# The rows of ten units by way of DRAM instead of one-hot products

## The chip, the cores and the metric

The kernel runs on one core of a Trainium2 chip. The metric is the time of one execution on the device, in microseconds, as the median of several runs. TensorE multiplies matrices, VectorE and ScalarE work on elements, GpSimd (POOL) does the same more slowly and issues the indirect DMAs, SyncE (SP) issues most of the other transfers. 16 DMA engines move the data of all queues.

## The reference

Two blocks follow each other on 512 tokens of 1024 channels. Each has a mixer and then a mixture of experts. The change is in the first block's mixture: 32 experts in four groups, two experts of one group for each token.

```python
def hier_moe(x2d, w_grp, b_grp, w_exp, b_exp, w_gate, w_up, w_down):
    ...
    combine = jnp.sum(jax.nn.one_hot(global_idx, N_EXPERTS, dtype=jnp.float32) * weights[..., None], axis=1)
    y = jnp.zeros_like(x2d)
    for e in range(N_EXPERTS):
        h = jax.nn.silu(x2d @ w_gate[e]) * (x2d @ w_up[e])
        y = y + combine[:, e:e + 1] * (h @ w_down[e])
    return y
...
xn = rmsnorm(h, norm_ffn_g[l]).reshape(B * S, D)
y = hier_moe(xn, ...)
h = h + y.reshape(B, S, D)
```

## The kernel before

The kernel runs in four stages: `mixer1`, `moe1`, `mixer2`, `moe2`. The tokens' sum `h` stays in SBUF as four tiles of [128 tokens, 1024]. A build step gives each engine one fixed order of its instructions. It takes those that are ready first, by a model of their times, so an instruction may stand well ahead of its place in the text; `in_order` keeps the written order for some stretches.

**The first mixture** (`moe1`, L1626). Two experts are one unit; there are 16 units. An expert has 64 slots, a unit 128. The routing (`route`, `tables`) leaves for each slot the number of its token (`mo.num` as float32, `mo.idx` as an integer) and its weight (`mo.wts`); empty slots have a number out of range. In `body` (L1646) a unit does this:

- `gather` (L1578): GpSimd issues an indirect DMA that fetches the tokens' normed rows from DRAM (`xd`) into one of two tiles `xg`, two units ahead.
- `gathered`: TensorE transposes them, ScalarE copies them out (`xTh`).
- The hidden layer (L1673): 64 products with the weights of gate and up, then Silu and a product (`hh`), transposed again by `turned`.
- `down` (L1633), one unit late: 16 products (L1641) with the down weights into PSUM. `rows_hl` (L1736) evicts them, times the slots' weights, as a high part on ScalarE and a low part on VectorE; `onehot` (L1741) makes the matrix slot by token.
- `scatter` (L1746): the rows of two units go to `h`, one half of the columns in each of two later units: 16 products with the one-hot matrices (`scatter_mm`, L1759 and L1760) and four adds on `h` (L1753) for a half. In units 3 to 14 there is one such half each; what is left follows in and after the last unit.

The weights come in pieces of 1 MB, six for a unit (`moe_load`, L1526), in the order of use, into a ring of 17 places. SyncE issues a piece when the piece that had its place has been used. After the 16 units a loop does further rounds, if an expert has more than 64 tokens; ahead of it all engines meet. Then the last unit's rows are added (`end`), and the norms of the next block follow (`sums_two`).

**Where the second mixture has the like.** There, the rows of 14 units go to a DRAM array `yd` (L1828), and eight indirect DMAs (L1885) bring them back into SBUF at the end; `places` (L1419) makes the row numbers. The first mixture does not call it.

**The first mixer.** `mixer1` (L438) loads the projections' weights piece by piece on SyncE (`wload`, L282), and the LoRA weights `lw` (L528). In step P0 of its list `sb_proj` (L635) makes `qz`, and GpSimd clears half of the partitions of each half of it (L638, L639).

Of the kernel before, what the change touches and what calls it, by code (L numbers as in the profile page):

```python
# [8 lines left out]
F32 = mybir.dt.float32  # L9
# [7 lines left out]
T = 512  # L17
D = 1024
NT = 4
# [7 lines left out]
BYDRAM = 14  # L27
ZROW = BYDRAM * 96
# [3 lines left out]
def drain(gen):  # L32
    """what a generator returns"""
    while True:
        try:
            next(gen)
        except StopIteration as e:
            return e.value


class Layout:
    """Columns of the packed constant arrays, one array per part of the program."""
# [19 lines left out]
    "mo1": (("cap64", 8), ("sl64", 128), ("g_f1", 8)),  # L62
    "mo2": (("cap96", 8), ("sl96", 128), ("g_f2", 8), ("row", 16)),
# [3 lines left out]
def host_consts(inp):  # L67
# [27 lines left out]
    # numbers of tokens, less 4096, as sums of two that bfloat16 holds  # L95
# [3 lines left out]
    put("row", one * np.where(np.arange(16) < BYDRAM, 96 * np.arange(16), 1e5))  # L99
# [22 lines left out]
def pieces(w, width=256):  # L122
    """[1024, n*width] -> [n, 128, 8*width], row d = k*128+p."""
    w = np.asarray(w)
    d, n = w.shape
    return np.ascontiguousarray(
        w.reshape(d // 128, 128, n // width, width).transpose(2, 1, 0, 3)).reshape(n // width, 128, -1)
# [50 lines left out]
class Kern:  # L178
# [16 lines left out]
    def act_set(self, name, after=None):  # L195
        """switch ScalarE's function table; what follows on ScalarE stays behind it"""
# [12 lines left out]
    def in_order(self):  # L209
        """every engine issues what is written here in the order in which it is written"""  # L210
# [19 lines left out]
    def cbf(self, pool, name):  # L230
        """a constant in bfloat16"""
# [21 lines left out]
    def psum(self, **banks):  # L253
        """new division of the 8 PSUM banks"""
# [12 lines left out]
    def ps_names(self, **names):  # L267
        """further names, each for banks in turn"""
# [6 lines left out]
    def rot(self, tags):  # L275
        """the next bank from a cycle of tags"""
# [8 lines left out]
    def wsplit(self, pool, t, w, bufs=2, eng=None):  # L285
        """a piece [128, 8, w] as hi + lo"""
# [11 lines left out]
    def proj_plan(self, w, order):  # L298
        """pieces of the weights that projections will ask for"""
# [27 lines left out]
    def rsqrt(self, pool, dst, src, scale, eps, tag):  # L327
        """dst = (src*scale + eps)^-0.5"""
# [5 lines left out]
    def to_dT(self, n, xn, xh, xl, diag=None, halfway=None):  # L334
        """a tile [128 tok, d], times a diagonal if there is one, transposed as hi + lo"""
# [21 lines left out]
    def norm_in(self, pool, pp, x, xh, xl):  # L357
        """rmsnorm of the input, transposed, and the first projection: of its first half while the second is on its way"""
# [27 lines left out]
    def sums_two(self, room, junk):  # L386
        """What norm_two needs. With w = h*g1 and a = mean(h^2) + eps, the result is w*g2*(mean(w^2) + eps*a)^-0.5.
        GpSimdE and VectorE take two tiles each; for GpSimdE's, the factors go on diagonals.
        room: a [128, 2 * d] for each tile of tokens, for w, and w*g2; junk: another"""
# [33 lines left out]
    def norm_two(self, xh, xl):  # L423
        """rmsnorm(rmsnorm(h)*g1)*g2, transposed"""
# [3 lines left out]
    def norm_h(self, pool):  # L428
        """h = rmsnorm(h)*g1, the first block's output"""
# [8 lines left out]
    def mixer1(self, after):  # L438
# [51 lines left out]
        # P projections and A attention of a pair of heads, R a unit of RWKV-7: one's products fill the other's waits  # L490
        for step in "R00 R01 P0 R10 R11 A0 P1 R20 R21 A1 P2 R30 R31 A2 P3 A3".split():
            kind, j = step[0], int(step[1])
            if kind == "P":
                qkv[j] = self.sb_proj(pp, sp, j, xh, xl)
                if j == 3:
# [20 lines left out]
    def wo_load(self, w):  # L516
        """the output projection's weights, in the ring of the mixture that follows: pieces on their way"""
# [5 lines left out]
    def mixer1_rw_in(self, bp, wk, pp, first, xh, xl, AR, bt, kt, vch, xg, TTc, PC, lora):  # L523
# [34 lines left out]
        for j in range(4):  # L558
# [8 lines left out]
            # key  # L567
# [19 lines left out]
            # k*(1+(a-1)*k_a)  # L587
# [4 lines left out]
            # receptance  # L592
# [5 lines left out]
            # L = strict(A~ b~^T), transposed blocks  # L598
# [9 lines left out]
        # (I - L)^-1 of 128 32x32 matrices, one per lane  # L608
# [15 lines left out]
    def to_tok(self, pool, p, dst, tag):  # L624
        """channel-major psum [128 ch, 512 tok] -> token-major [128, NT, 128]"""
# [54 lines left out]
    def blocks(self, scores, weighted):  # L680
        """the blocks of queries, the scores of one ahead of the products of the one before"""
# [6 lines left out]
    def weighted(self, tp, tags, b, w, v, ot):  # L688
        """ot[2 heads x 64, block b] = (w v)^T for weights [128 tok, keys]"""
# [18 lines left out]
    def head_norm(self, tp, tags, ot, dst, g):  # L708
        """rmsnorm of [2 heads x 64, 512 tok] over each head's channels"""
# [9 lines left out]
    def rw_unit(self, up, n, g, S, o, AR, bt, kt, vch, xg, g2, TTc, PC):  # L719
        """RWKV-7 for 128 tokens of 4 heads (2 pairs); in three steps: what needs no state, the chain, the output"""  # L720
# [9 lines left out]
        # products, s on partitions  # L730
# [21 lines left out]
        # token-major copies  # L752
# [24 lines left out]
        # [W | U0]  # L777
# [10 lines left out]
        # R' = R~ + M_rb W (transposed), M = I + W^T b~  # L788
# [15 lines left out]
        # chain over the 4 chunks  # L804
# [23 lines left out]
        # group norm, bonus, gate  # L828
# [32 lines left out]
    def out_mm(self, st, d, n, k, hl, first, last):  # L861
        """one row chunk of the product for 128 tokens and 256 columns, into half a bank"""
# [22 lines left out]
    def out_start(self, o, wo, ks, rest, tags, cx):  # L885
        """three quarters of the output projection's columns over the rows that are there already"""
# [21 lines left out]
    def out_finish(self, st, tag, trtag, rtags):  # L908
        """the rest of the output projection; with the last columns rmsnorm(h) to DRAM, and the routing"""
# [99 lines left out]
        with self.tc.issue_after(ins.ins):  # L1009
# [4 lines left out]
            if mo.which == 2:  # L1014
                self.places(mo.rp, mo)

# [1 line left out]
    def mixer2(self, after):  # L1018
# [28 lines left out]
        self.yd = tc.dram_tile([ZROW + 1, D], F32, name="yd2")  # L1047
        for j in range(4):
# [8 lines left out]
            if j == 3:  # L1057
                nc.sync.dma_start(self.yd[ZROW:ZROW + 1], qkv[1][65:66].rearrange("p h t -> p (h t)"))
# [13 lines left out]
    def lower_bound(self, ap):  # L1072
        """first row of the softmax over the two rows of logits, and one minus it"""
# [13 lines left out]
    def sigmoid(self, dst, p):  # L1087
        """dst = 1/(1+exp(-p)) with exp and log alone"""
# [6 lines left out]
    def fox_gate(self, ap, xh, xl):  # L1095
        """running sum of minus the log forget gates, [8 heads, 512 tok]"""
# [13 lines left out]
        # -log_sigmoid(x) = max(-x, 0) + log(1 + exp(-|x|))  # L1110
# [12 lines left out]
    def hgrn_head(self, hp, pp, j, xh, xl, o, lb):  # L1123
        """HGRN2 of one head (128 channels), 128 tokens a step"""
# [35 lines left out]
        # blocks of 8: reference halfway between the ends  # L1160
# [13 lines left out]
        # pairs of half blocks: reference at the boundary  # L1174
# [12 lines left out]
        # state terms  # L1187
# [44 lines left out]
    def fox_proj(self, tp, pp, j, xh, xl):  # L1232
        """two heads; row 64 of the keys is for the gates' sums"""
# [16 lines left out]
    def fox_attn(self, tp, j, qkv, o, tags):  # L1250
        """forgetting attention of two heads"""
# [27 lines left out]
    def route(self, rp, mo, a, b, lg, cb, sb):  # L1279
        """Tiles a to b of tokens: top-1 group, top-2 experts of it, and the places in the experts' lists.  # L1280
        cb, sb: PSUM banks for the counts, and what the slots hold. A generator that stops after each step of VectorE."""
# [8 lines left out]
        def first(vals, w, mx, ix):  # L1290
            """maximum, and its first place less 64"""
# [13 lines left out]
        # the other groups' experts out of the way  # L1305
# [13 lines left out]
        # tokens before this one, per expert  # L1319
# [12 lines left out]
    def weigh(self, mo):  # L1332
        """the weights of the tokens' experts"""
# [659 lines left out]
```

## Time and profile before

| what | value |
|---|---|
| time, median of 3 runs | 1439.21 us (1439.2 to 1443.11) |
| span of the profiled execution | 1440.1 us, 0.9 us above the median |
| TensorE busy | 1329.5 us, 92% |
| VectorE busy | 891.8 us, 62% |
| ScalarE busy | 700.5 us, 49% |
| GpSimd busy | 390.2 us, 27% |
| moved by DMA | 273.53 MB, 190 GB/s in the mean |

The page cuts the span into 40 slices of 36 us. The first mixture lies at about 460 to 735 us, slices 12 to 20. A share of busy time over the whole span mixes stages with different limits; a stage is read from the view of its own stretch. A granted clock of 1.00 is TensorE at 2.4 GHz, 0.5 is 1.2 GHz.

### The profile page before, as it was taken

The page shows a single profiled execution, that of the slowest core. Times are in us where ns is not written, and L with a number is a line of the kernel's source. Part 1 is how long each engine was busy: PE and PEld are TensorE (multiplying, and loading weights), DVE is VectorE, ACT ScalarE, POOL GpSimd, SP SyncE. Part 2 cuts the span into 40 slices and gives each one's busy share as a digit, 9 for nine tenths or more (in the row PEclk, how much of TensorE's full clock was granted, in tenths as well). Part 3 has the DMA queues.
Part 4 walks back from the last instruction along what each step waited for, and adds up shares of the span by engine and source line. Part 5 has one row for each costly group of instructions (what it writes and reads, how often), then busy time and mean ns, then how long its engine had stood idle before and what let it go on. Part 6 is the DMA issues. An engine that isn't in the chain of part 4 may idle for free. (4 is left out here: it accounts for less than half of the span.)

```text
span 1440.1 us, 20831 instructions
## 1 busy us (share of the span) xinstructions
PE 1329.5 (92%) x7952; PEld 954.6 (66%) x7952; DVE 891.8 (62%) x1498; ACT 700.5 (49%) x1217; POOL 390.2 (27%) x311
## 2 busy tenths in 40 slices
PE   7999999989997999999959899999896999999994
PEld 5776766757696556555528677767795666666662
DVE  4578856575745123323255847565747799999995
ACT  6433433333644212111144555555634788888883
POOL 1010224331104000000047201010223555555555
PEclk9999999999998999999989999999997999999997
DMA  5222100000584999998122111201385899889943
GB/s 186 74 88 74 52 16 1 1 1 2 226 325 166 407 422 422 422 417 346 42 74 72 59 47 57 73 31 34 130 356 199 280 367 373 320 339 395 380 177 147
DMA packets 49286, 273.53 MB, mean 190 GB/s; under 512 B 7497, under 2 KB 8393, under 8 KB 23570
## 3 DMA queue, kind: packets, MB, share of 16 engines
q1 hardware_dynamic: 41058, 249.48, 45.4%
q0 software_dynamic: 7248, 21.24, 4.2%
q10 hardware_dynamic: 864, 1.31, 0.3%
q8 instruction: 66, 1.08, 0.3%
q14 instruction: 50, 0.41, 0.1%
HBM read 266.48 MB, written 11.80 MB: 193 GB/s over the span
## 5 line engine op out<-in xcount | busy, mean ns | idle before, releaser
L1608 DVE TENSOR_TENSOR elo<-ew,ehi 128x1024 fp32r<-128x1024 f32 x147 | 231.3, 1615 | 31.9 <-ACT ehi L1607 23.1
L1607 ACT ACTIVATE ehi<-ew 128x1024 fp32r<-128x1024 f32 x192 | 203.0, 1060 | 61.8 <-PE ua L1855 42.3
L317 PE MATMUL mm<-xh,whi 128*128 128x512 f32 (+1 forms) x384 | 156.6, 408 | 4.0 <-DVE hq L1134 3.7
L317 PE MATMUL mm<-xh,wlo 128*128 128x512 f32 (+1 forms) x384 | 153.3, 399 | 0.0
L317 PE MATMUL mm<-xl,whi 128*128 128x512 f32 (+1 forms) x384 | 152.9, 398 | 0.5 <-DVE xl L349 0.3
L1608 POOL TENSOR_TENSOR elo<-ew,ehi 128x1024 fp32r<-128x1024 f32 x45 | 126.0, 2803 | 63.9 <-ACT ehi L1607 62.2
L1673 PE MATMUL mm<-ew,xTh 128*64 128x256 f32 x1024 | 120.0, 386 | 0.0
L1856 PE MATMUL ua<-elo,xTh 128*96 128x512 f32 x256 | 102.8, 402 | 8.4 <-DVE elo L1608 8.4
L1854 PE MATMUL ua<-ehi,xTh 128*96 128x512 f32 x256 | 101.9, 398 | 0.7 <-ACT xTh L1596 0.6
L1579 POOL DMA_INDIRECT xg<-xd,idx x32 | 36.6, 1145 | 242.7 <-PE sb L1592 153.3
L1855 PE MATMUL ua<-ehi,xTl 128*96 128x512 f32 x256 | 101.6, 397 | 0.0
L1673 PEld LDWEIGHTS mm<-ew,xTh 128*64 128x64 f32 x1024 | 73.6, 139 | 41.9 <-issue 8.0
L291 ACT ACTIVATE whi<-w 128x1024 fp32r<-128x1024 f32 x53 | 55.9, 1056 | 86.7 <-PE mm L317 68.0
L292 DVE TENSOR_TENSOR wlo<-w,whi 128x1024 fp32r<-128x1024 f32 x52 | 64.1, 1234 | 52.4 <-ACT whi L291 51.0
L317 PEld LDWEIGHTS mm<-xh,whi 128*128 128x128 f32 x384 | 73.8, 192 | 23.0 <-DVE hq L1134 5.3
L317 PEld LDWEIGHTS mm<-xl,whi 128*128 128x128 f32 x384 | 73.7, 192 | 16.3 <-issue 3.0
L317 PEld LDWEIGHTS mm<-xh,wlo 128*128 128x128 f32 x384 | 73.4, 191 | 16.3 <-issue 2.6
L1676 ACT ACTIVATE hh<-mm 128x256 f32<-128x256 f32 x16 | 6.1, 383 | 128.9 <-PE mm L1673 128.9
L1677 DVE TENSOR_TENSOR hh<-hh,mm 128x256 f32<-128x256 f32 x16 | 6.7, 421 | 95.1 <-ACT hh L1676 95.1
L1641 PE MATMUL ua<-ew,hT 128*64 128x512 f32 x240 | 65.3, 600 | 0.0
L1856 PEld LDWEIGHTS ua<-elo,xTh 128*96 128x96 f32 x256 | 41.8, 163 | 30.4 <-DVE elo L1608 11.2
L1738 ACT ACTIVATE oh<-ua,wts 128x512 fp32r<-128x512 f32 x30 | 20.6, 687 | 72.9 <-PE ua L1641 72.9
(632 smaller groups left out, 3160.9 us busy)
## 6 DMA issues: line engine op xcount, KB each, us to landing
ew<-in_e1up_dram SPq DMA_DIRECT2D x32, 1024.0 KB, 15.2
ew<-in_e2up_dram SPq DMA_DIRECT2D x32, 1024.0 KB, 11.2
ew<-in_e2gate_dram SPq DMA_DIRECT2D x32, 1024.0 KB, 9.9
ew<-in_e2down_dram SPq DMA_DIRECT2D x32, 1024.0 KB, 11.7
ew<-in_e1gate_dram SPq DMA_DIRECT2D x31, 1024.0 KB, 17.8
ew<-in_e1down_dram SPq DMA_DIRECT2D x30, 1024.0 KB, 16.3
w<-in_win_dram SPq DMA_DIRECT2D x53, 512.0 KB, 3.5
ew<-in_wout_dram SPq DMA_DIRECT2D x8, 1024.0 KB, 7.2
```

The lines of the kernel that those rows point to most:

```text
L291: nc.scalar.activation(hi, s, AF.Copy)
L292: (eng or nc.vector).tensor_tensor(lo, s, hi, OP.subtract)
L317: mm = lambda w, x, start=False, stop=False: nc.tensor.matmul(p[:, s], w[:, k], x[:, k, s], start=start, stop=stop, skip_group_check=parts ...
L1579: return self.nc.gpsimd.indirect_dma_start(out=xg, out_offset=None, in_=mo.xd, in_offset=bass.IndirectOffsetOnAxis(ap=idx[:, u:u + 1], axi ...
L1607: self.hi = nc.scalar.activation(hi, s, AF.Copy)
L1608: self.lo = (nc.gpsimd if pool else nc.vector).tensor_tensor(lo, s, hi, OP.subtract)
L1641: nc.tensor.matmul(p[hs(a)], hT[:, k, hs(a)], w[a][:, k * 1024 + d * 512:k * 1024 + d * 512 + 512], start=k == 0, stop=k == 1)
L1673: nc.tensor.matmul(d[hs(a)], xT[:, k, hs(a)], w[2 * m + a][:, k * 256:k * 256 + 256], start=k == 0, stop=k == KD - 1)
L1738: self.last = self.nc.scalar.activation(oh, p, AF.Copy, scale=w)
L1854: nc.tensor.matmul(p, xh[:, kk], hi[:, s], start=kk == 0, stop=False)
L1855: nc.tensor.matmul(p, xl[:, kk], hi[:, s], start=False, stop=False)
L1856: nc.tensor.matmul(p, xh[:, kk], lo[:, s], start=False, stop=kk == KD - 1)
```

## The change

The rows of units 0 to 9 of the first mixture no longer go to `h` by one-hot products. ScalarE evicts them, times their weights, as float32 (`by_dram`), and GpSimd writes them by an indirect DMA to a new DRAM array of 1280 rows, a row for each slot of the first 20 experts; the row number of an empty slot is out of range. In unit 10, after the tenth of these writes, eight indirect DMAs fetch for each token its first and then its second expert's row and add it onto `h` while they land; a token whose expert is not among the 20 has a number out of range. Units 10 to 15 keep the one-hot products in the same places as before. `places` is now called for the first mixture too and makes both lists of row numbers. The array is filled with zeros by one DMA on SyncE, written at step P0 of the first mixer, from 64 cleared partitions of `qz`. The high and the low part of evicted rows become one tile. Further rounds stay as they were. The diff also takes out comments, which are not shown.

```diff
-BYDRAM = 14
-ZROW = BYDRAM * 96
+BYDRAM = {1: 20, 2: 14}
+CAP = {1: 64, 2: 96}
+ZROW = {k: BYDRAM[k] * CAP[k] for k in CAP}
...
             if kind == "P":
                 qkv[j] = self.sb_proj(pp, sp, j, xh, xl)
+                if j == 0:
+                    self.yd = tc.dram_tile([ZROW[1], D], F32, name="yd1")
+                    zeros = qkv[0][0][64:128, 0]
+                    nc.sync.dma_start(self.yd.rearrange("(p a) (d c) -> p (a d) c", p=64, c=T),
+                                      zeros[:, None, :].to_broadcast([64, ZROW[1] // 32, T]))
...
-            if mo.which == 2:
-                self.places(mo.rp, mo)
+            self.places(mo.rp, mo)
...
-        nc.vector.tensor_scalar(mo.row, rw, float(ZROW), None, op0=OP.min)
+        if mo.which == 2:
+            nc.vector.tensor_scalar(mo.row, rw, float(ZROW[2]), None, op0=OP.min)
+            return
+        nc.vector.tensor_copy(mo.row, rw)
+        ot = rp.tile([128, mo.U], F32, name="rot")
+        nc.vector.tensor_scalar(ot, mo.num, 4096.0, 1e5, op0=OP.is_ge, op1=OP.mult)
+        nc.vector.tensor_tensor(mo.out, ot, self.c("out1"), OP.add)
...
+        def by_dram(u, hT):
+            w = [self.moe_next(mo) for _ in range(2)]
+            ot = yp.tile([128, D], F32, tag="o1", name="ot", bufs=3)
+            for d in range(2):
+                nc.scalar.activation(ot[:, 512 * d:512 * d + 512], product(hT, w, d), AF.Copy, scale=mo.wts[:, u:u + 1])
+            nc.gpsimd.indirect_dma_start(
+                out=self.yd, out_offset=bass.IndirectOffsetOnAxis(ap=mo.out[:, u:u + 1], axis=0), in_=ot, in_offset=None,
+                bounds_check=ZROW[1] - 1, oob_is_err=False)
...
+            far = BYDRAM[1] // 2 if first else 0
...
-                if u > 2:
-                    e = (u - 3) // 2 * 2
+                if u > far + 2:
+                    e = (u - 3 - far) // 2 * 2
                     self.scatter(ys[e:e + 2], (u + 1) % 2)
-                if prev:
+                if prev and prev[0] < far:
+                    by_dram(*prev)
+                elif prev:
                     ys.append(down(*down_args(*prev, num, wts)))
+                if far and u == far:
+                    for c in range(2):
+                        for n in range(NT):
+                            nc.gpsimd.indirect_dma_start(
+                                out=self.h[:, n], out_offset=None, in_=self.yd,
+                                in_offset=bass.IndirectOffsetOnAxis(ap=mo.row[:, n, c:c + 1], axis=0),
+                                bounds_check=ZROW[1] - 1, oob_is_err=False, compute_op=OP.add)
```

## Rows read from the trace of the kernel before

**Rows 1.** The page's part 2: GB/s moved in 40 slices of 36 us.
```profile
GB/s 186 74 88 74 52 16 1 1 1 2 226 325 166 407 422 422 422 417 346 42 74 72 59 47 57 73 31 34 130 356 199 280 367 373 320 339 395 380 177 147
```
**Rows 2.** Stretches: busy us (instructions) by engine, granted clock, DMA share, GB/s.
```profile
480.00:500.00 20.00, 20.00 (x152) 11.13 (x150) 2.34 (x4) 5.09 (x10) 1.98 (x2) 1.00 1.01 420
...
700.00:720.00 20.00, 20.00 (x88) 9.90 (x89) 6.95 (x10) 3.02 (x5) 0.00 (x0) 1.00 0.00 1
```
**Rows 3.** TensorE in order of time, one unit: start us, us, line, out<-in, xcount.
```profile
533.20 7.13 PE L1673 MATMUL mm<-ew,xTh 128*64 128x256 f32 x64
540.25 1.09 PE L1592 MATMUL sb<-pc_c,xg 128*128 128x128 f32 x8
541.10 0.48 PE L1759 MATMUL ch<-oh,SC 128*128 128x512 f32 x1
...
545.09 3.65 PE L1641 MATMUL ua<-ew,hT 128*64 128x512 f32 x16
548.68 0.44 PE L1718 MATMUL sb<-pc_c,hh 128*128 128x128 f32 x2
549.05 7.13 PE L1673 MATMUL mm<-ew,xTh 128*64 128x256 f32 x64
```
**Rows 4.** TensorE's longest wait, 440 to 740 us: total, times, longest.
```profile
PE ua L1641 <- DMA ew<-in_attn_g_dram: 5.6, 1, 5.6
```
**Rows 5.** Queues of transfers, 480 to 640 us: packets, MB, share of 16 engines.
```profile
q1 hardware_dynamic: 8809, 64.15, 95.8%
q0 software_dynamic: 1728, 3.12, 5.2%
```
**Rows 6.** The same, GpSimd's queue, 440 to 740 us.
```profile
q0 software_dynamic: 2736, 7.35, 6.6%
```
**Rows 7.** L1523: landing of the pieces issued at 572.1 and at 616.2 us.
```profile
L1523 SPq DMA_DIRECT2D ew<-in_e1gate_dram x1: 327/327/327, 572.1 to 572.1; - x1
...
DMA to landing us min/median/max: 18.1/18.1/18.1
...
DMA to landing us min/median/max: 16.3/16.3/16.3
```
**Rows 8.** TensorE in time: hidden layers of units 10 and 13, last product.
```profile
612.50 4.10 PE L1673 MATMUL mm<-ew,xTh 128*64 128x256 f32 x34
...
669.60 0.65 PE L1673 MATMUL mm<-ew,xTh 128*64 128x256 f32 x2
...
729.26 0.38 PE L1718 MATMUL sb<-pc_c,hh 128*128 128x128 f32 x2
```
**Rows 9.** SyncE's issues in order of time, 14 to 60 us.
```profile
14.70 0.33 SPq L282 DMA_DIRECT2D w<-in_win_dram  x1
21.73 0.33 SPq L528 DMA_DIRECT2D lw<-in_lora_dram  x1
```
**Rows 10.** GpSimd in order of time, 0 to 60 us.
```profile
1.00 0.52 POOL L638 MEMSET qz<- 64x512 f32 x1
```
**Rows 11.** TensorE in order of time, 30 to 75 us.
```profile
31.01 1.02 PE L551 MATMUL ua<-wa,lw 128*128 128x512 f32 x2
```
**Rows 12.** VectorE's instructions by line, 1095 to 1125 us: busy us, mean ns.
```profile
L1426 DVE TENSOR_TENSOR rwm<-M,pc_mo 128x128 f32<-128x128 bf16 x1 | 0.3, 276 | 0.0
```
**Rows 13.** VectorE in order of time at the mixture's start, with the wait before.
```profile
476.25 0.42 DVE L1677 TENSOR_TENSOR hh<-hh,mm 128x256 f32<-128x256 f32 x1 [10.11 <-ACT hh L1676]
```
**Rows 14.** Gathers of tokens (L1579), 480 to 640 us: duration ns min/median/max.
```profile
L1579 POOL DMA_INDIRECT xg<-xd,idx x11: 988/988/991, 485.8 to 632.1; - x11
...
DMA to landing us min/median/max: 7.9/8.2/9.7
```
**Rows 15.** The second mixture's gathers from `yd` (L1885): landing.
```profile
DMA to landing us min/median/max: 5.2/5.5/5.6
```
**Rows 16.** TensorE in order of time: two waits, with what ended them.
```profile
805.89 0.79 PE L317 MATMUL mm<-xh,whi 128*128 128x512 f32 x1 [2.92 <-DVE hq L1134]
...
1209.89 0.47 PE L1856 MATMUL ua<-elo,xTh 128*96 128x512 f32 x1 [1.39 <-DVE elo L1608]
```
**Rows 17.** The stretch of the first of these waits, columns as in rows 2.
```profile
805.00:810.00 5.00, 4.11 (x12) 3.31 (x13) 4.96 (x10) 2.93 (x5) 0.00 (x0) 0.66 0.19 70
```

More of the change, by code (lines that the diff above doesn't have):

```diff
@@ L61 @@
     "mo": (("io64", 64), ("tok", 8), ("upb", 128)),
-    "mo1": (("cap64", 8), ("sl64", 128), ("g_f1", 8)),
-    "mo2": (("cap96", 8), ("sl96", 128), ("g_f2", 8), ("row", 16)),
+    "mo1": (("cap64", 8), ("sl64", 128), ("g_f1", 8), ("row1", 32), ("out1", 16)),
+    "mo2": (("cap96", 8), ("sl96", 128), ("g_f2", 8), ("row2", 16)),
 })
@@ L98, in host_consts @@
     put("g_f1", cols(inp["norm_ffn_g"]))
-    put("row", one * np.where(np.arange(16) < BYDRAM, 96 * np.arange(16), 1e5))
+    for k, e in (1, np.arange(32)), (2, np.arange(16)):
+        put("row%d" % k, one * np.where(e < BYDRAM[k], CAP[k] * e, 1e5))
+    put("out1", i[:, None] + 128 * np.arange(16))
     put("g_f2", cols(inp["ffn_norm_2"]))
@@ L1046, in mixer2 @@
         self.ps_names(ha=("ua",), ho=("ch",), fz=("pq", "sb", "sb"))
-        self.yd = tc.dram_tile([ZROW + 1, D], F32, name="yd2")
+        self.yd = tc.dram_tile([ZROW[2] + 1, D], F32, name="yd2")
         for j in range(4):
@@ L1057, in mixer2 @@
             if j == 3:
-                nc.sync.dma_start(self.yd[ZROW:ZROW + 1], qkv[1][65:66].rearrange("p h t -> p (h t)"))
+                nc.sync.dma_start(self.yd[ZROW[2]:ZROW[2] + 1], qkv[1][65:66].rearrange("p h t -> p (h t)"))
                 cP.close()
@@ L1426, in places @@
         nc.vector.tensor_tensor(tm.rearrange("p n c e -> p (n c) e"), mo.M.rearrange("p n c e -> p (n c) e"),
-                                self.c("row")[:, None, :].to_broadcast([128, 2 * NT, E]), OP.mult)
+                                self.c("row%d" % mo.which)[:, None, :].to_broadcast([128, 2 * NT, E]), OP.mult)
         nc.vector.tensor_reduce(rw, tm, AX.X, OP.add)
@@ L1481, in moe_open @@
         mo.extra = mo.keep.tile([1, 1], I32, name="extra")
-        mo.row = mo.keep.tile([128, NT, 2], I32, name="row") if which == 2 else None
+        mo.row = mo.keep.tile([128, NT, 2], I32, name="row")
+        mo.out = mo.keep.tile([128, mo.U], I32, name="out") if which == 1 else None
         self.upb = self.cbf(mo.keep, "upb")
@@ L1631, in moe1, with product @@
         hs = lambda a: slice(64 * a, 64 * a + 64)
+        def product(hT, w, d):
+            p = self.ps("dn")
+            for k in range(2):
+                for a in range(2):
+                    nc.tensor.matmul(p[hs(a)], hT[:, k, hs(a)], w[a][:, k * 1024 + d * 512:k * 1024 + d * 512 + 512],
+                                     start=k == 0, stop=k == 1)
+            return p
+        def by_dram(u, hT):
[6 more added lines that the diff above has]
+                bounds_check=ZROW[1] - 1, oob_is_err=False)
         def down(hT, w, wt, SC):
@@ L1636, in down @@
             for d in range(2):
-                hl.append([yp.tile([128, 512], R32, name=nm + str(d), bufs=2 + d) for nm in ("oh", "ol")])
-                p = self.ps("dn")
-                for k in range(2):
-                    for a in range(2):
-                        nc.tensor.matmul(p[hs(a)], hT[:, k, hs(a)], w[a][:, k * 1024 + d * 512:k * 1024 + d * 512 + 512],
-                                         start=k == 0, stop=k == 1)
-                self.rows_hl(*hl[d], p, wt)
+                y = yp.tile([128, 2, 512], R32, tag="o%d" % d, name="oh%d" % d, bufs=2 + d)
+                hl.append([y[:, 0], y[:, 1]])
+                self.rows_hl(*hl[d], product(hT, w, d), wt)
             return SC, hl
@@ L1664, in body @@
                 if last:
-                    self.scatter(ys[12:14], 0)
+                    self.scatter(ys[12 - far:14 - far], 0)
                     ys.append(down(*down_args(*prev, num, wts)))
@@ L1689, in body @@
                 prev = u, hT
-            self.scatter(ys[12:15], 1)
-            self.scatter(ys[14:15], 0)
+            self.scatter(ys[12 - far:15 - far], 1)
+            self.scatter(ys[14 - far:15 - far], 0)
             if not first:
@@ L1876, in body @@
                     if prev and not last:
-                        y = down(*prev, num, wts, not first or prev[0] >= BYDRAM, turned)
+                        y = down(*prev, num, wts, not first or prev[0] >= BYDRAM[2], turned)
                     else:
@@ L1887, in body @@
                                 in_offset=bass.IndirectOffsetOnAxis(ap=mo.row[:, n, c:c + 1], axis=0),
-                                bounds_check=ZROW, oob_is_err=False)
+                                bounds_check=ZROW[2], oob_is_err=False)
                 g = self.moe_slot(mo)[:, 0:D]
```

## The prediction

> **What bounds the kernel now.** I read the profile from the whole to the single unit: the transfer line of the page [rows 1], the stretches of the first mixture [rows 2], TensorE's order of work in one unit [rows 3], what TensorE waited for [rows 4], and then the transfers of the same stretch [rows 5 to 7]. The reader is to see two resources that are both full. In each stretch from 480 to 720 us TensorE is busy 20.00 of 20 us at the full granted clock, 2.4 GHz [rows 2]. A unit takes 549.05 - 533.20 = 15.85 us: the hidden layer's products to 540.25, transposes to 541.10, sixteen scatter products from 541.10 to 545.09 (3.99 us), the down projection to 548.68 [rows 3]. In the whole mixture the longest wait of TensorE is 5.6 us, and it comes after the last product, where all engines meet ahead of the loop [rows 4]. Read alone, this says that a product removed is time gained.
>
> But the transfers of 480 to 640 us take 95.8% + 5.2% of the 16 engines [rows 5]. From these rows come the two prices of the sum. The weights' queue moved 64.15 MB, which is 61.2 pieces of 1.049 MB: 0.958 x 160 / 61.2 = 2.505 us each. The gathers' queue moved 3.12 MB, 762 rows of 4 KB: 0.052 x 160 / 762 = 0.0109 us of all engines for a row (0.175 us of one). Over the mixture the gathers moved 7.35 MB less three weight pieces, 4.2 MB or 1026 rows, 64 for each unit [rows 6]: empty slots of the 128 are not moved. So a unit needs 6 x 2.505 + 64 x 0.0109 = 15.7 us of transfers, and TensorE takes 15.85. **The two run level.** What TensorE lives on is a lead: a gate piece of unit 10 was issued at 572.1 and landed 18.1 us later, at 590.2 [rows 7], and unit 10 began at 612.5 [rows 8], 22.3 us after it. Towards the end the lead grows: the last down piece of unit 11 landed at 616.2 + 16.3 = 632.5 [rows 7], so unit 13's gate pieces, two places behind it, landed at about 637.7 (2.62 us each with their share of gathers), and unit 13 began at 669.6 [rows 8]. From there to the last product, 729.6, are 60.0 us.
>
> **What the change removes.** For the first ten units the scatter products go: ten halves of 3.99 us, 39.9 us of TensorE. The scatter of units 10 to 14 stays where it was, from unit 13 on. With them go ten one-hot tiles, twenty low parts and forty adds of VectorE, which was no bound. A unit of these costs TensorE 15.85 - 3.99 = 11.9 us. ScalarE's evictions stay in number.
>
> **What it adds to the transfers.** Ten writes of about 64 rows: 640 x 0.0109 = 7.0 us of all engines. With them a unit needs 15.7 + 0.7 = 16.4 us, 4.5 more than TensorE does; the lead of 22 us is used up after some five units, near unit 8, and from then on TensorE waits for weights. The gather-adds read the same 640 rows and add them onto h. No row shows a transfer that adds. At a plain row's price they cost 7.0 us. As h has to be read too, I set the upper bound at two rows, 14.0 us, and take 10.5. A gather-add cheaper than a plain row is excluded, since it moves the same row.
>
> **Where TensorE ends.** Unit 13's gate pieces land at 637.7 + 7.0 + 10.5 = 655.2 (652 to 659) in place of 637.7, and there TensorE is waiting for them. Of the 60.0 us that followed, one half of units 10 and 11 (3.99 us) is free of these weights and may go into the wait ahead; between none and both halves, I take one. The last product then ends at 655.2 + 60.0 - 4.0 = 711 instead of 729.6: **18.5 us earlier**, with bounds of 10.5 (14.0 for the adds, nothing moved forward) and 26 (7.0, both halves). What is late next is the weights; VectorE, the sync ahead of the loop and all behind it only shift.
>
> **The zeros.** 1280 rows, 5.24 MB in pieces of 2 KB, go out on SyncE's queue. In the program this stands at step P0, after fourteen of the first mixer's 26 weight pieces; from slice 3 on the page has 74 GB/s and less [rows 1], and there it would cost nothing. But its source is ready at 1.5 us [rows 10]: GpSimd's clearing of qz was drawn forward to the start, and so can this transfer be, to behind the third weight piece, when SyncE has nothing else to issue until 14.70 [rows 9]. The loads ahead of it are eight of 512 KB and two tables of constants, 4.7 MB or 11.3 us at the weights' 418 GB/s [rows 5] from about 2 us on, so it starts at about 13.5. At the same rate it takes 12.5 us; at most a 2 KB piece costs what a 4 KB row does, 2560 x 0.0109 = 28 us. Behind it on the queue are a weight piece (14.70) and the LoRA weights (21.73), 1.25 us each, which then land between 28.5 and 44; TensorE's first product with them began at 31.0 [rows 11]. The wait is 0 to 13 us. The middle of the two prices is 20 us and a wait of 5.5; as another projection could stand ahead, I take **4 us later**.
>
> The Trainium skill, SBUF — State Buffer, section Door 1 (the DMA port swizzle), says that 64 partitions reach half of the 16 ports and measures 196 GB/s; the zeros come from 64 partitions, so by that page they would take some 27 us and TensorE's wait would be about 12, with the sum at 1433. No row here shows a transfer from 64 partitions.
>
> **Small edits.** The table of places adds eight small operations of VectorE, at 0.3 us or less each [rows 12], before the first write that needs them; VectorE waits 10.1 us for ScalarE ahead of its first product in the mixture [rows 13], and this hides them (2.4 us if the cover were gone). GpSimd issues 18 indirect DMAs more, 1 us each [rows 14]; it has little else here. A write waits for ScalarE's two evictions, and the gather of a later unit's tokens may queue behind it, some 5 us later than now; it has one unit and a hidden layer, over 19 us, against a landing of 8.2 us [rows 14].
>
> **Sum.** 1440.1 - 18.5 + 4.0 = 1425.6 for the profiled execution, which is 0.9 us above the median of the runs: 1424.7, so 1425. The bounds of the terms (for the zeros 0 to 5.5) give 1413 to 1434 for this case alone.
>
> **Rivals.**
> - *All 39.9 us come off*: 1403 with the zeros at 4. For it: TensorE never waited for weights [rows 4]. Against it: ten units at 4.5 us need a lead of 45 us, and there are 22. 6 in 100.
> - *The zeros cost 13 us*: 1434, between 1427 and 1440 with the other bounds. 17 in 100.
> - *The gather-adds hold up GpSimd (slower)*. The second four add onto the same rows of h as the first four, so they wait for their landing, and GpSimd with them; behind them may stand the gather for unit 13. The write of unit 9 lands at about 621 (its weights at 607, the product, two evictions, 8.2 us of landing). With R for four gather-adds from issue to landing, unit 13 starts at 621 + 2R + 10. It is hidden under the weights to R = 12; from R = 17 the kernel is slower than before (with the zeros' 4 us). 320 rows alone take 3.5 us, at half the engines beside the weights 7, with two rows' price 14; one gather from such rows lands in 5.5 us with little beside it [rows 15]. At R = 25 it would be 1454. Against it: unit 13's slots come free at its predecessor's transposes, ahead of the down projection that the write waits for, so its gather can be issued first. 15 in 100.
> - *TensorE's clock falls in the waits*. After a wait of 2.92 us a product took 0.79 us [rows 16], and the granted clock of that stretch was 0.66, partly 1.2 GHz [rows 17]; and after a wait of 1.39 us the next product took 0.47 [rows 16]. Units 8 to 12 would wait 4.5 us each, in parts. If all their products ran at half speed, a unit would take up to 23.8 us against 16.4, and five units lose 37; but then it no longer waits, which brings the clock back, so I take half: about 1443. Against it: the wait is split over three pairs of pieces, near 1.5 us each. 5 in 100. [...]
>
> **How the numbers follow.** The forecast has 52 in 100, the four rivals 43; 5 are left for an order of instructions that I do not see. A measurement of this kernel tells about 0.3%, 4.3 us, from no change. Faster by more than that (below 1434.9): nearly all of the forecast (50), the first rival (6), half of the second (9), 2 of the rest: 67. Within it: 2, 8, 2 of the third and 3 of the clock: 15. Slower: 13 of the third, 2 of the clock, 3 of the rest: 18. The range is 1411 to 1444: it leaves out the first rival and the forecast's lowest end (9) and the third rival's upper part with the rest (11).
>
> **What would show it.** Right: transfers at 420 GB/s to about 700 us; TensorE waiting for weights from unit 8 on; unit 13 starting at 650 to 660; the last product of the mixture at about 711, plus the start's shift. The zeros: SyncE's issue near 6 us and the first LoRA product later than 31.0. Wrong: units of 11.9 us to the end (the first rival); TensorE waiting for the tokens of unit 13, and GpSimd for h (the third); a granted clock below 1 between 560 and 650. If the transfers fell below 420 GB/s while weights were outstanding, the price of a row was wrong.

## The result: slower by 1.5%

| what | before | after |
|---|---|---|
| time, median | 1439.2 us | 1461.24 us (1460.48 to 1462.95) |
| ratio, 95% interval | | 1.0146 (1.0133 to 1.0159) |
| span of the profiled execution | 1440.1 us | 1458.8 us |
| TensorE busy | 1329.5 us | 1308.3 us |
| moved by DMA | 273.53 MB | 284.12 MB |

The forecast was 1425 us, faster; the kernel became 22 us slower. TensorE is busy 21 us less and the span is 19 us longer, so some 40 us of new idle time have to be found. The profile shows three places.

**The start.** SyncE's issues in order of time, 14 to 60 us, which answer to [rows 9]:

```profile
15.10 0.63 SPq L502 DMA_DIRECT2D yd<-qz  x1
21.63 6.51 SPq L537 DMA_DIRECT2D lw<-in_lora_dram  x1
```

TensorE's first LoRA product, which answers to [rows 11], and its next long wait:

```profile
46.27 2.05 PE L560 MATMUL ua<-wa,lw 128*128 128x512 f32 x2 [9.77 <-DMA w<-in_win_dram]
...
59.77 0.50 PE L321 MATMUL sb<-xh,whi 128*128 128x512 f32 x1 [4.19 <-ACT whi L295]
```

The profile puts the first wait down to a weight piece; the product reads the LoRA weights, which stand one place ahead of that piece on the queue. The second wait is for ScalarE, which has been busy with the results of the LoRA products since 48.35 us and splits the next piece only behind them:

```profile
58.68 1.04 ACT L295 ACTIVATE whi<-w 128x1024 fp32r<-128x1024 f32 x1
```

Seven stretches: busy us (instructions) of TensorE, its weight loads, VectorE, ScalarE and GpSimd, then granted clock, DMA share, GB/s, as in [rows 2]:

```profile
20.00:40.00 20.00, 16.15 (x89) 13.62 (x88) 5.98 (x8) 6.91 (x9) 0.71 (x3) 1.00 0.96 207
40.00:60.00 20.00, 9.55 (x17) 4.01 (x18) 2.42 (x3) 9.16 (x13) 0.20 (x1) 0.74 0.31 100
...
590.00:595.00 5.00, 5.00 (x32) 2.82 (x29) 0.00 (x0) 0.01 (x1) 0.00 (x0) 0.66 1.02 421
600.00:620.00 20.00, 18.74 (x122) 9.52 (x122) 0.42 (x1) 4.57 (x9) 4.06 (x4) 1.00 1.02 419
640.00:660.00 20.00, 15.68 (x96) 7.86 (x94) 1.93 (x3) 3.12 (x6) 7.88 (x5) 0.96 1.03 380
660.00:680.00 20.00, 16.39 (x70) 8.08 (x66) 3.20 (x5) 3.12 (x6) 5.71 (x4) 0.84 1.04 338
680.00:700.00 20.00, 17.25 (x92) 9.38 (x92) 4.59 (x8) 0.98 (x2) 0.00 (x0) 0.77 1.01 404
```

The zeros did move forward to the start. From 20 to 40 us the DMA engines are 96% busy and carry only 207 GB/s, half of what they carry at 600 us with about the same share (102%); the LoRA product begins at 46.3 in place of 31.0, and TensorE works 9.55 of the 20 us after 40, in part at 1.2 GHz (mean clock 0.74).

**The mixture.** TensorE in order of time: the first hidden layer of the kernel before, and then, after the change, the first hidden layer, that of unit 13, the last product and the first one behind the meeting ahead of the loop, which answer to [rows 8]:

```profile
466.49 1.12 PE L1673 MATMUL mm<-ew,xTh 128*64 128x256 f32 x4
```

```profile
485.58 0.70 PE L1706 MATMUL mm<-ew,xTh 128*64 128x256 f32 x2
...
673.75 0.65 PE L1706 MATMUL mm<-ew,xTh 128*64 128x256 f32 x2
...
742.98 0.38 PE L1760 MATMUL sb<-pc_c,hh 128*128 128x128 f32 x2
752.22 1.12 PE L1654 MATMUL ua<-ew,ew 128*64 128x512 f32 x2 [8.86 <-issue]
```

It begins 19.1 us late (485.6 against 466.5). From its first hidden layer to its last product it takes 257.8 us against 263.1: only 5.3 us are gained. Unit 13 begins 188.2 us after the first hidden layer, where the prediction has 655.2 - 466.5 = 188.7; but from there to the last product it is 69.6 us, where the prediction has 56.0. Ahead of the loop TensorE then waits 8.86 us in place of 5.6 [rows 4].

**The adds.** GpSimd in order of time: the first gather-add, the eighth, and the gather of unit 15's tokens; in brackets the wait before and what ended it:

```profile
645.60 1.61 POOL L1725 DMA_INDIRECT h<-yd,row  x1 [9.52 <-DMA yd<-ot,out]
...
669.09 1.56 POOL L1725 DMA_INDIRECT h<-yd,row  x1 [2.35 <-DMA h<-yd,row]
670.96 1.02 POOL L1595 DMA_INDIRECT xg<-xd,idx  x1 [0.30 <-PE ua L1654]
```

While they run, the transfers fall from 419 to 380 and 338 GB/s with all DMA engines busy, as the stretches above show. TensorE's waits from 440 to 780 us (total, times, longest), where [rows 4] had one of 5.6:

```profile
PE mm L1706 <- DMA ew<-in_e1up_dram: 10.0, 6, 3.8
...
PE pq L1801 <- DVE h L1795: 3.6, 3, 3.0
PE ch L1801 <- DVE h L1795: 2.7, 1, 2.7
```

So the waits are for weights, for `h`, which VectorE can't touch until the adds have landed, and ahead of the loop. The adds also come to GpSimd at a higher price than the prediction's 1 us: 1.55 to 1.61 us each.

### The profile page after: what moved, and what is told of

It reads as the page before. It is cut to its first block, busy times and chain, and to the rows that moved or that the text cites. A ratio compares the mean times of both kernels' runs of the same rounds, so it can differ in the third digit from the quotient of the medians.

```text
span 1458.8 us, 20514 instructions
## 1 busy us (share of the span) xinstructions
PE 1308.3 (90%) x7792; PEld 932.5 (64%) x7792; DVE 845.3 (58%) x1436; ACT 701.4 (48%) x1217; POOL 411.5 (28%) x329
## 2 busy tenths in 40 slices
DMA packets 54452, 284.12 MB, mean 195 GB/s; under 512 B 8803, under 2 KB 9699, under 8 KB 28738
## 5 line engine op out<-in xcount | busy, mean ns | idle before, releaser
L1706 PE MATMUL mm<-ew,xTh 128*64 128x256 f32 x1024 | 127.9, 399 | 10.7 <-DMA ew<-in_e1up_dram 10.0
L321 PEld LDWEIGHTS mm<-xh,whi 128*128 128x128 f32 x384 | 73.5, 191 | 22.7 <-DVE hq L1142 5.4
L1595 POOL DMA_INDIRECT xg<-xd,idx x32 | 36.8, 1150 | 178.2 <-PE sb L1608 94.7
L321 PEld LDWEIGHTS mm<-xl,whi 128*128 128x128 f32 x384 | 73.7, 192 | 16.3 <-issue 3.0
L321 PEld LDWEIGHTS mm<-xh,wlo 128*128 128x128 f32 x384 | 73.3, 191 | 16.4 <-issue 2.6
L1654 PE MATMUL ua<-ew,hT 128*64 128x512 f32 x240 | 71.8, 601 | 2.2 <-DMA ew<-in_e1down_dram 2.2
L1166 POOL TENSOR_TENSOR hAT<-hAT,hmt 128x512 f32<-128x512 f32 x16 | 22.1, 1381 | 117.4 <-DVE hmt L1165 116.8
```

What stands on the lines that cost most here:

```text
L321: mm = lambda w, x, start=False, stop=False: nc.tensor.matmul(p[:, s], w[:, k], x[:, k, s], start=start, stop=stop, skip_group_check=parts ...
L1595: return self.nc.gpsimd.indirect_dma_start(out=xg, out_offset=None, in_=mo.xd, in_offset=bass.IndirectOffsetOnAxis(ap=idx[:, u:u + 1], axi ...
L1654: nc.tensor.matmul(p[hs(a)], hT[:, k, hs(a)], w[a][:, k * 1024 + d * 512:k * 1024 + d * 512 + 512], start=k == 0, stop=k == 1)
L1706: nc.tensor.matmul(d[hs(a)], xT[:, k, hs(a)], w[2 * m + a][:, k * 256:k * 256 + 256], start=k == 0, stop=k == KD - 1)
```

## Experiments at the start

**The zeros later.**

```diff
-                if j == 0:
+                if j == 2:
...
-                    zeros = qkv[0][0][64:128, 0]
+                    zeros = qkv[2][0][64:128, 0]
```

> The changed kernel with one edit: the zeros are written at step P2 of the first mixer and read from the qz of that step, which is not there before step A0 is done, so the transfer can't be drawn forward to the start. Theory (the zeros at the start cost the whole 19 us by which the first mixture begins later): the first LoRA product is back at about 31 us in place of 46.3, the first hidden layer of the mixture begins at about 466.5 in place of 485.6, and the time is 1461 - 19 = 1442 us (1438 to 1446). Rival (half of the 19 us comes from another order of the products that the build chose): about 1451. The mixture itself stays as it is, 258 us from its first hidden layer to its last product.

Measured: 1443.71 us, ratio to before 1.0016 (1.0005 to 1.0027). The 17.5 us come back, and the first LoRA product is where it was:

```profile
30.05 1.02 PE L560 MATMUL ua<-wa,lw 128*128 128x512 f32 x2
```

The mixture begins at 466.9 and takes 258.8 us. Even so, with zeros that cost nothing, the kernel is no faster than before. The zeros now go out at 162.5 us, where hardly anything else moves, and are as slow there, at some 205 GB/s. The transfers of 160 to 190 us, in 40 slices:

```profile
GB/s 0 0 0 164 339 251 210 210 202 205 205 208 202 202 210 199 216 202 208 218 205 202 208 208 202 213 208 205 205 202 208 202 205 210 197 210 205 202 216 254
```

Contention was therefore not what made them slow; they only cost nothing there.

**The zeros alone, in the kernel before.** The five added lines of step P0, nothing else of the change.

> The kernel before with the zero fill alone, at the same place and from the same 64 partitions as in the changed kernel; no write, no gather-add. Theory (the zeros alone cost the start's 19 us): 1439 + 19 = 1458 us (1454 to 1462), and the first LoRA product at about 46 us. Rival (what was lost at the start needs the rest of the change): under 1448.

Measured: 1458.78 us, ratio 1.0120 (1.0103 to 1.0137). One transfer that nobody reads makes the kernel before 17 us slower:

```profile
45.33 2.05 PE L556 MATMUL ua<-wa,lw 128*128 128x512 f32 x2 [8.80 <-DMA w<-in_win_dram]
```

**The same zeros from 128 partitions.**

```diff
-                    zeros = qkv[0][0][64:128, 0]
+                    zeros = sp.tile([128, 320], F32, name="zz", bufs=1)
+                    nc.gpsimd.memset(zeros, 0.0)
```

> The changed kernel with the same 5.24 MB of zeros at the same place, but from 128 partitions of a tile of their own, in pieces of 1280 bytes (for a tile of 2 KB a partition there is no room). Theory A (64 partitions feed only part of the engines at full rate): the 5.24 MB take about 13 us in place of some 23, the first LoRA product begins at some 36 us in place of 46.3, and the time is about 1450 us (1446 to 1454). Theory B (the volume and the pieces' number cost, wherever they come from): 23 us or more as before, since a piece of 1280 bytes is no cheaper than one of 2 KB, and 1461 us (1457 to 1470).

Measured: 1450.88 us, ratio 1.0065 (1.0048 to 1.0081), 10.4 us less than the changed kernel, as theory A has it. GB/s of 15 to 40 us in 40 slices, the changed kernel first, then this one:

```profile
GB/s 0 170 184 177 351 387 370 324 236 206 200 203 206 200 210 206 210 200 210 200 200 210 203 203 203 210 206 233 187 197 216 213 203 210 197 210 206 210 203 206
```

```profile
GB/s 105 52 125 288 377 395 393 397 393 393 393 395 395 393 397 403 395 397 395 417 369 377 389 393 393 424 419 424 422 419 419 361 33 26 0 0 0 0 0 0
```

The same bytes at the same place go at 393 in place of 205 GB/s, though in smaller pieces, and the LoRA product begins at 35.3. The source's 64 partitions set the rate.

## Experiments in the mixture

All of these start from z_late, so that the start is out of the way.

**No gather-adds.** The statement in unit 10 is left out.

> The kernel of z_late without the eight gather-adds: it leaves out the rows of units 0 to 9 in the sum h, which are written to DRAM and not fetched. Theory (the adds take some 15 us of all transfer engines from the weights and hold VectorE and TensorE up by some 6 us more): the mixture, 258 us from its first hidden layer to its last product, becomes 243 (240 to 248), and the time is that of z_late less 14 us (10 to 18), about 1428. Rival (the adds are beside the point, the weights alone bound units 7 to 13): within 5 us of z_late. With the prediction's price for the adds alone it would be 10.5 us.

Measured: 1427.45 us, ratio 0.9897 (0.9880 to 0.9913); 16.3 us below z_late. Two stretches with the columns of [rows 2]:

```profile
600.00:620.00 20.00, 17.65 (x116) 9.10 (x117) 0.42 (x1) 4.47 (x9) 4.06 (x4) 1.00 1.02 419
...
660.00:680.00 20.00, 20.00 (x134) 11.08 (x133) 5.14 (x10) 3.47 (x7) 0.00 (x0) 1.00 1.01 420
```

and the GpSimd queue of 480 to 640 us, which answers to [rows 5]:

```profile
q0 software_dynamic: 3226, 5.96, 9.8%
```

The transfers go at 418 to 420 GB/s to 680 us, and up to unit 13 TensorE waits in short pieces only, of 1.8 us at most, with the clock at 2.4 GHz. Units 8 to 11 begin 16.6 to 17.1 us apart: the transfers set the pace, without the adds too. The ten writes, with one gather of tokens more than before in this window, are what (9.8% - 5.2%) x 160 = 7.4 us of all engines is; without that gather it is some 6.7.

**The same rows without the addition.**

```diff
-                                bounds_check=ZROW[1] - 1, oob_is_err=False, compute_op=OP.add)
+                                bounds_check=ZROW[1] - 1, oob_is_err=False)
```

> The kernel of z_late with the eight indirect transfers onto h without the addition: the same rows come from the same places to the same places and overwrite h (the sum of the block's input and of units 0 to 9 is left out). Theory A (the addition itself doubles the price of a row, 327 against 159 ns of one engine): the packets take 160 ns, the 640 rows 7 us of all engines in place of 13, POOL and VectorE wait about half as long for their landing, and the time is that of z_late less 8 us, 1436 (1432 to 1439). Theory B (the place of the transfers and the waits around h cost, whatever the transfer does): within 3 us of z_late, 1441 to 1446.

Measured: 1432.64 us, ratio 0.9954 (0.9937 to 0.9970), 11.1 us below z_late. From its first hidden layer to its last product the mixture takes 251.0 us against 258.8, so 7.8 us come from the adds, as theory A has it; it also begins 2.9 us earlier (464.0 against 466.9), and why was not looked for. GpSimd's queue with the addition (z_late, 628 to 672 us), then without (624 to 664 us):

```profile
q0 software_dynamic: 1290, 2.90, 32.3%
```

```profile
q0 software_dynamic: 1306, 2.91, 18.8%
```

0.323 x 44 = 14.2 us of all engines with it, 0.188 x 40 = 7.5 us without, for the same rows (both with one gather of tokens among them). **The addition doubles the price of a row.** The adds lengthen the mixture from 242.4 us in no_adds to 258.8: 7.8 us are the addition, 8.6 the plain rows with the waits for their landing.

**Four units in place of ten.** `BYDRAM = {1: 8, 2: 14}`.

> The kernel of z_late with units 0 to 3 by DRAM in place of 0 to 9; the gather-adds stand in unit 4. Theory (the lead of the weights pays for some five units, and no more): four units at 4 us less each, 16 us of TensorE, and 8 us more of transfers; unit 13 could begin at 669.6 - 16 = 654 and its weights land at 637.7 + 8 = 646, so TensorE never waits for weights, all 16 us come off, and with 3 us more at the loop and 2 behind it the time is 1439 - 11 = 1428 us (1424 to 1434). Rival (each unit by DRAM is worth the same, and ten gave nothing): 1438 to 1444.

Measured: 1461.15 us, ratio 1.0136 (1.0110 to 1.0163): 33 us worse than expected. TensorE's longest wait, and the issues of GpSimd ahead of it:

```profile
PE sb L1608 <- DMA xg<-xd,idx: 23.5, 1, 23.5
```

```profile
533.53 1.61 POOL L1725 DMA_INDIRECT h<-yd,row  x1 [7.53 <-DMA yd<-ot,out]
...
553.80 1.56 POOL L1725 DMA_INDIRECT h<-yd,row  x1 [2.24 <-DMA h<-yd,row]
555.67 1.02 POOL L1595 DMA_INDIRECT xg<-xd,idx  x1 [0.30 <-issue]
```

This is the prediction's third rival, in a kernel in which I had not looked for it: the tokens of unit 7 are queued on GpSimd behind eight adds, four of which wait for landings. With ten units it is unit 15's gather that stands there, which has time.

**The second four adds two units later, with four units.** `u == far` becomes `u - far in (0, 2)`, with c = 0 and c = 1.

> The kernel of far4 with the first experts' four gather-adds in unit 4 as there and the second experts' four in unit 6; on GpSimd the gather of unit 7's tokens then stands between the two fours, and nothing is left out. Theory (the second four hold GpSimd up, since each waits for the landing of one of the first): the wait of 23.5 us for unit 7's tokens goes, TensorE may wait some us for h where the first scatter comes, and the time is that of far4_no_adds plus 2 to 10 us, about 1431 (1426 to 1438). Rival (the tokens land late because of the adds' own transfers, whatever the order): still some 15 us or more of wait for tokens, 1450 or more.

Measured: 1447.41 us, ratio 1.0039 (1.0029 to 1.0050).

```profile
PE sb L1608 <- DMA xg<-xd,idx: 9.1, 2, 8.5
```

The order on GpSimd was worth 15 of the 23.5 us. The gather, issued at 542.4 now, still landed only after 15.7 us where it takes 8.2 beside the weights without adds [rows 14], so the rival holds for the rest, and with it the time lies between the two.

**Four units without adds.**

> The kernel of far4 without its eight gather-adds; it leaves out the rows of units 0 to 3 in h. In far4 TensorE stood still for 23.5 us at 548.4, for the tokens of unit 7, whose gather GpSimd could issue only behind the eight adds. Theory (the lead of the weights pays for four units, and only the adds' hold on GpSimd spoilt far4): no such wait, all 16 us of scatter products come off, 1440 - 16 = 1424 us (1420 to 1431), though six units fewer than in no_adds (1427) go by DRAM. Rival (the wait has another cause, or the products don't come off): over 1435.

Measured: 1434.05 us, ratio 0.9947 (0.9930 to 0.9963): less than the 16 us of removed products, though TensorE has no wait of 1 us from the first hidden layer to the last. So the lead does pay for four units, and the 16 us did come off: unit 7 begins 16.0 us earlier than before (548.9 against 564.9). Then units 7 to 9 take 60.7 us where the kernel before takes 47.6. TensorE's down products by form over the mixture, count, busy us and mean ns, before and here:

```profile
L1641 PE MATMUL ua<-ew,hT 128*64 128x512 f32 x240 | 65.3, 600 | 0.0
```

```profile
L1654 PE MATMUL ua<-ew,hT 128*64 128x512 f32 x240 | 71.7, 601 | 0.0
```

The same 240 products are busy 6.4 us longer: of the 16 us that leaves 9.6, and the mixture is 9.4 us shorter than before (253.7 against 263.1). Unit 7's, in order of time:

```profile
580.57 0.59 PE L1654 MATMUL ua<-ew,hT 128*64 128x512 f32 x1
580.78 0.38 PE L1706 MATMUL mm<-ew,xTh 128*64 128x256 f32 x1
581.00 1.45 PE L1654 MATMUL ua<-ew,hT 128*64 128x512 f32 x3
...
583.19 3.65 PE L1654 MATMUL ua<-ew,hT 128*64 128x512 f32 x12
```

In [rows 3] sixteen take 3.65 us as one group. Here the first is parted from the next three by a product of the hidden layer, and the twelve behind them take 3.65 us alone. The kernel before has this form too, but only from unit 10 on, and there its units begin 17.7 to 22.7 us apart, without a wait of 1 us, instead of 15.85; here, and in the kernels with ten units, it begins with unit 6. The products of a unit's two experts seem to run side by side only in the first order; this was read from the rows and not tested.

**The adds in unit 14.**

```diff
-                if far and u == far:
+                if far and u == 14:
```

> The kernel of z_late with the eight gather-adds written in unit 14 in place of unit 10. Theory (the adds cost what they take from the weights, which have landed by about 690 us): the mixture up to unit 13 runs as in no_adds, the adds go out at 685 to 715 us beside few weights, and the time is 1427 plus 0 to 5: 1430 us (1426 to 1436). Rival (the adds' landing holds up h, so VectorE and TensorE wait wherever they stand): 1440 to 1446, with waits of VectorE for h in the last unit.

Measured: 1443.01 us, ratio 1.0021 (1.0010 to 1.0031): the rival. VectorE, then TensorE, in order of time:

```profile
702.15 0.69 DVE L1795 TENSOR_TENSOR h<-h,pq 128x512 f32<-128x512 f32 x1 [13.88 <-DMA h<-yd,row]
```

```profile
702.89 0.79 PE L1801 MATMUL pq<-oh,SC 128*128 128x512 f32 x1 [11.02 <-DVE h L1795]
```

Up to unit 13 the mixture ran as in no_adds. Then the adds and VectorE's adds of the last units took turns on `h`, and TensorE stood behind VectorE. The build drew the adds forward: seven of the eight were issued from 655 to 676 us, beside the last weights, and not at 685 to 715, so the theory's own condition was not met in this run.

**Fourteen units by DRAM, adds in unit 14.** `BYDRAM = {1: 28, 2: 14}`, and the scatter of pairs that no longer exist left out.

> The kernel of z_late with units 0 to 13 by DRAM and the gather-adds in unit 14; unit 14 and 15 keep the one-hot products. Theory (up to unit 13 the weights set the pace, and the products behind them can go, since then transfers are idle): against adds_u14 another 16 us of TensorE come off, nearly all behind unit 13, against 3 us more of writes; 1418 us (1411 to 1425). Rival (the adds now land last: their first needs the row of unit 13, about 690, and they take 2 times 10 us or more, and the last units' rows wait for h): 1428 to 1438.

Measured: 1438.54 us, ratio 0.9986 (0.9976 to 0.9996), the upper end of the rival. The same wait, in the middle of the last hidden layer:

```profile
PE ch L1802 <- DVE h L1796: 18.9, 2, 18.8
```

**The same, with nothing that needs h ahead of the loop.** Unit 14's evicted rows go to two places of the ring, and their products join those of unit 15:

```diff
-                self.scatter([y], d, [n], ("so", "gu", "so", "dn"))
+                self.scatter([self.kept, y] if first else [y], d, [n], ("so", "gu", "so", "dn"))
```

> The kernel of far14 with unit 14's evicted rows kept in two places of the ring, and its one-hot products done with those of unit 15 behind the loop. In far14 TensorE waited 18.8 us, in the middle of unit 15's hidden layer, for VectorE, and VectorE for the landing of the adds onto h. Theory (that wait has no work behind it that needs h): it goes, the down products of unit 15 begin at some 710 in place of 728, the end has 4 us of products more, and the time is 1438.5 - 19 + 4 = 1424 us (1418 to 1431). Rival (the meeting ahead of the loop or the last adds on h take the wait over): 1433 to 1439.

Measured: 1429.20 us, ratio 0.9912 (0.9892 to 0.9932), 0.9% faster than before and the fastest of the kernels that leave nothing out. The theory had 1424; the rival has a part of it, since most of the wait moved on, to the meeting ahead of the loop:

```profile
720.74 1.98 PE L1654 MATMUL ua<-ew,ew 128*64 128x512 f32 x4 [22.16 <-issue]
```

GpSimd's last add was issued at 709.0. To see whether its landing holds the meeting, the last run leaves the adds out:

> The kernel of far14_end without its eight gather-adds; it leaves out the rows of units 0 to 13 in h. Theory (in far14_end the meeting of the engines ahead of the loop waits for the landing of the last gather-add, issued at 709.0, and TensorE with it for 22.2 us at 698.6): TensorE's wait ahead of unit 15's down products falls to the 5.6 to 9 us that it is in the other kernels, they begin at some 705 to 708 in place of 720.7, and the time is 1429 - 14 = 1415 us (1411 to 1419). Rival (the meeting waits for something else, the loop's code or SyncE's loads): the wait stays above 15 us and the time at 1424 or more.

Measured: 1413.47 us, ratio 0.9800 (0.9780 to 0.9820), and

```profile
703.87 1.97 PE L1654 MATMUL ua<-ew,ew 128*64 128x512 f32 x4 [5.75 <-issue]
```

It does: 15.7 us of adds lie open there, although no weights are left to be delayed (up to its last product the mixture takes 231.2 us with the adds and 231.1 without).

## Why the prediction was wrong

| term | foretold | by the runs |
|---|---|---|
| scatter products off, writes on | -29.0 | -14.1 (no_adds against before) |
| gather-adds | +10.5 (7 to 14) | +16.3 (z_late less no_adds) |
| zeros | +4 (0 to 5.5) | +17.5 (after less z_late) |
| sum | -14.5 | +19.7 |

The measured change is +22.0; the 2 us between are those by which the two groups of runs of the kernel before differ (1439.2 and 1441.5).

Two steps failed by about as much, the zeros (13.5 us) and the worth of the scatter (14.9), and the adds by 5.8. No one of them turned the sign: with the zeros alone at their measured price the sum is -1.0, with the zeros alone as foretold it is +6.2.

- **What bounds the kernel** was right. A unit without scatter takes 12.0 us (foretold 11.9); TensorE waits for weights from unit 7 on (foretold 8), at 420 GB/s; the writes cost some 6.7 us (7.0). The first rival, all 39.9 us off, is out. That unit 13 began where it was foretold, 188.2 us after the first hidden layer, is luck: without adds it took 182.3 in place of 178.2, and a part of the adds came only behind it. Three readings of mine were off, and nothing hangs on them: the unit of 15.85 us holds for units 3 to 9 alone, TensorE is busy 19.80 and 19.95 of 20 us in the stretches from 640 to 680, and the loads ahead of the zeros are 4.6 MB and not 4.7.
- **The zeros.** That they would move to the start, ahead of the LoRA weights, was foretold and happened, though SyncE issued them at 15.10 and not near 6. The failed step is the price: I took the middle between the weights' rate and 28 us, then a wait of 5.5 and of that 4. The transfer went at 205 GB/s, some 26 us, near the upper end. Nor did I look at what stands behind the LoRA products. In this trace 9.77 us of waiting at the LoRA product, 4.2 us for the split piece that ScalarE makes behind it, and products at 1.2 GHz make up most of it. The second rival was nearer, with 13 us and 17 in 100, and still too small. By the Trainium skill, SBUF — State Buffer, section Door 1 (the DMA port swizzle), the sum would have been 1433. The trace agrees with that page: it states 196 GB/s for 64 partitions in a transfer of 1 MiB, this one of 5.24 MB went at some 205 with nothing beside it, and 128 partitions gave 393. A price that a page states, near one of my two bounds, deserved more weight than their middle.
- **The gather-adds.** The mechanism was right, that they take transfers from the weights, and their size was the term of two rows, my upper bound: 14.2 us of all engines. What was missing altogether is `h`, since VectorE was only to shift: VectorE can't add on it until the adds have landed, and TensorE's banks wait for VectorE (6.3 us here, 11 in adds_u14, 18.8 in far14).
- **The scatter's worth.** From the first hidden layer to unit 13's I had 178.2 us without adds (644.7 - 466.5); no_adds takes 182.3, since from unit 7 to 13 the units begin 16.7 us apart in the mean and not 16.4, and TensorE waits from unit 7 on. The half of units 10 and 11 that was to go into the wait, 4.0 us, gained nothing: from unit 13 to the last product it is 60.1 us as before. What was only to shift did not: ahead of the loop are 3.2 us more, in the starting point of the mixture 2.3 and behind the loop 2.0. That is 15.7 us together, against 29.0 - 13.2 = 15.8 between the two profiled executions.
- **The rivals on GpSimd and the clock.** With ten units GpSimd's queue held up no tokens that were needed, although the rival's R was 23.5 us (from the first add's issue to the eighth's, which waits for the fourth to land): only unit 15's gather stood behind them. With four units TensorE did wait for tokens, also for 23.5 us. The clock rival was true in part. In no_adds the clock stayed at 2.4 GHz with waits of up to 1.8 us. In the changed kernel a wait of 1.95 us for weights, well ahead of the adds, was followed by 5 us at a mean of 0.66:

```profile
589.60 5.14 PE L1706 MATMUL mm<-ew,xTh 128*64 128x256 f32 x29 [1.95 <-DMA ew<-in_e1up_dram]
```

Around the waits of up to 3.8 us that came with the adds the mean fell to 0.84 and 0.77. Unit 13 took 30.9 us there against 21.3 in no_adds; 5.7 of the 9.6 us are the waits for `h`, and what the clock has of the rest was not measured by itself.

Left open: why the wait ahead of the loop is 8.7 to 9.1 us in the kernels with ten units by DRAM and 5.4 to 5.8 before, in those with four and in far14_end_no_adds with fourteen; and the 2 us behind the loop. Neither was tried.

## What to carry to other kernels

A fill that "costs nothing" is priced at its place in the built order and with everything behind it on its queue; where nobody needs it for nearly 500 us, tie it to a place where transfers are idle. Where transfers and TensorE run level, work moved from TensorE to transfers is worth little more than the lead of the weights, here the scatter of four units (16 us; by unit 13 it was 20.8 us with ten). A transfer that lands on a tile makes every engine that writes this tile wait, so let nothing on the critical engine need the tile until the transfer is down.

## What was not expected of the hardware

- From 64 partitions the DMA engines moved some 205 GB/s, at the start and where nothing else ran, from 128 at the start 393, and showed themselves over 90% busy at the lower rate too (96% from 20 to 40 us).
- An indirect row that adds took 4.9 us of all engines for a MB (14.2 us for 2.90 MB), a plain one 2.6 (7.5 for 2.91).
- Sixteen half-array products took 3.65 us in one order, and twelve of them as long in another.
